# Rotary embedding on one core: 8 MB tiles of sixteen sequence rows per partition in place of 2 MB tiles of four

## Chip, cores, metric

One core of one Trainium2 chip runs the whole program. The metric is the device time of one execution in microseconds (us), as a median of several. The kernel before took 163.36 us (163.12 to 163.46, 4 runs). Profiled spans are 1.7 to 1.8 us shorter than the device time in every run whose record lists both; a span runs from the first to the last recorded instruction or transfer.

## The reference

The input x is [16, 512, 16, 64] (batch, sequence, head, dim) in float32, 33.55 MB. Only the first half of dim is rotated, by cos and sin tables of [512, 32], of which only the first 16 columns are used. The second half is copied.

```python
x1, x2 = x[..., :32], x[..., 32:]
c, s = cos[..., :16], sin[..., :16]          # broadcast over batch and head
first  = x1[..., :16] * c - x1[..., 16:] * s
second = x1[..., :16] * s + x1[..., 16:] * c
out = concatenate([first, second, x2], axis=-1)
```

33.55 MB must be read and 33.55 MB written. There are four vector products or sums per tile.

## The kernel before

One batch is one tile of 2 MB: sequence rows 4p to 4p+3 lie in partition p, so each partition's run in memory is 4 x 16 x 64 x 4 B = 16 KB. Six tiles can be resident. Products go to separate buffers `a_t` and `b_t`; the sums go back into the tile, and the tile is stored as it lies. The tables are expanded over heads by GpSimd at the start.

```python
x_pool  = tile_pool(name="xp",  bufs=6)      # 6 x 16 KB per partition
ab_pool = tile_pool(name="abp", bufs=4)
# ... GpSimd expands cos, sin to CCX, SSX [P, 4, H, 2, Q] ...
for b in range(B):                            # 16 tiles
    x_t = x_pool.tile([P, K, H, D], fp32)
    nc.sync.dma_start(out=x_t, in_=xf[b])                      # load, SP queue
    nc.vector.tensor_mul(out=a_t, in0=x12, in1=cc_op)          # 128 x 2048
    nc.vector.tensor_mul(out=b_t, in0=x12, in1=ss_op)          # 128 x 2048
    nc.vector.tensor_tensor(out=x12[.., 0:Q], in0=a_t[.., 0:Q], in1=b_t[.., Q:2*Q], op=subtract)  # 128 x 1024
    nc.vector.tensor_tensor(out=x12[.., Q:2*Q], in0=a_t[.., Q:2*Q], in1=b_t[.., 0:Q], op=add)     # 128 x 1024
    nc.scalar.dma_start(out=of[b], in_=x_t)                    # store, ACT queue
```

## Time and profile before

| | before |
|---|---|
| device time | 163.36 us |
| span | 161.4 us |
| bytes moved, mean rate | 67.25 MB, 417 GB/s |
| vector engine busy | 108.7 us (67%) |
| 2 MB load, median from issue to landing | 20.3 us |
| 2 MB store, the same | 23.4 us |

Lines of the page (the profiler's summary of one run) of before. DVE is the vector engine and POOL is GpSimd; SPq and ACTq are the queues from which loads and stores are issued; L64 is line 64 of the kernel. The issue of a DMA is when its queue starts it, its landing is when all of it has arrived. The lines are: busy time by engine, the rows of the span cut into 40 slices (a digit is the busy share in tenths; GB/s is what the DMA engines moved), two groups of vector instructions (busy us and mean ns of one, then the idle time before them), and the DMA issues (KB each, median us from issue to landing).

```profile
DVE 108.7 (67%) x64; POOL 6.0 (4%) x14
...
DVE  0009999999995692947839296592957939389400
...
DMA  5999999999999999999999999999999999999994
GB/s 162 430 414 447 414 382 443 414 430 447 418 434 434 422 443 430 418 451 422 426 443 422 430 434 430 434 434 418 447 422 426 451 414 428 439 422 438 430 422 195
...
L65 DVE TENSOR_TENSOR b_t<-x_t,SSX 128x2048 f32<-128x2048 f32 x16 | 36.5, 2283 | 0.0
L66 DVE TENSOR_TENSOR x_t<-a_t,b_t 128x1024 f32<-128x1024 f32 x16 | 19.5, 1220 | 0.2
...
x_t<-in_x_dram SPq DMA_DIRECT2D x16, 2048.0 KB, 20.3
out_dram<-x_t ACTq DMA_DIRECT2D x16, 2048.0 KB, 23.4
```

The DMA row is full from the second slice to the last but one, while the vector row has gaps. The table of windows (start:end, length, vector busy, GpSimd busy, clock, DMA share, GB/s) says at what rate:

```profile
5.00:6.00 1.00, 0.00 (x0) 0.00 (x0) 1.00 1.02 434
...
25.00:40.00 15.00, 14.93 (x10) 0.00 (x0) 1.00 1.00 430
...
140.00:150.00 10.00, 8.15 (x6) 0.00 (x0) 1.00 1.01 431
...
156.00:158.00 2.00, 0.00 (x0) 0.00 (x0) 1.00 0.95 410
```

It is about 430 GB/s with loads only (5 to 6 us), with both directions (25 to 150 us), and near that with stores only (156 to 158 us; the two windows before it have 451 and 426). 67.25 MB at 0.432 MB/us is 156 us of the 161.4 us span. The waits of the vector engine (engine, line, waited for: us in total, times, longest) are for loads and are short, but for the first one, of 11.9 us, which is for the expanded tables:

```profile
DVE a_t L64 <- DMA x_t<-in_x_dram: 30.1, 10, 3.2
DVE a_t L64 <- POOL CCX L49: 11.9, 1, 11.9
```

So the kernel is at the rate of the DMA engines, with a ramp at the start and a last landing at the end.

### The profile page before, as it was taken

How to read it: one execution, taken by the hardware profiler on the slowest of the kernel's cores; microseconds unless marked ns; L12 is line 12 of the kernel's file. 1: busy time of each engine (PE TensorE's matmuls, PEld its weight loads, DVE VectorE, ACT ScalarE, POOL GpSimd, SP SyncE). 2: the span in 40 equal slices, each digit the busy share in tenths (PEclk: the TensorE clock that was granted, in tenths of full speed). 3: DMA queues.
4: the chain of work that ended last, by engine and by line, in shares of the span. 5: the costliest groups of instructions: out<-in, count | busy, mean ns of one | idle time of the engine just before them, and what ended most of it. 6: DMA issues, size and time to landing. Idle time of an engine off the chain costs nothing.

```text
span 161.4 us, 189 instructions
## 1 busy us (share of the span) xinstructions
DVE 108.7 (67%) x64; POOL 6.0 (4%) x14
## 2 busy tenths in 40 slices
DVE  0009999999995692947839296592957939389400
POOL 3090000000000000000000000000000000000000
DMA  5999999999999999999999999999999999999994
GB/s 162 430 414 447 414 382 443 414 430 447 418 434 434 422 443 430 418 451 422 426 443 422 430 434 430 434 434 418 447 422 426 451 414 428 439 422 438 430 422 195
DMA packets 4673, 67.25 MB, mean 417 GB/s; under 512 B 544, under 2 KB 544, under 8 KB 576
## 3 DMA queue, kind: packets, MB, share of 16 engines
q1 hardware_dynamic: 2304, 33.56, 49.4%
q10 hardware_dynamic: 2304, 33.56, 48.5%
q0 software_dynamic: 64, 0.13, 0.2%
q14 instruction: 1, 0.01, 0.0%
HBM read 33.69 MB, written 33.55 MB: 417 GB/s over the span
## 4 chain that ended last, share of the span: by engine, by line
DMA 60%; DVE 28%; POOL 2%; issue 2%; DVEq 1%; POOLq 0%; SPq 0%; PEldq 0%
DMA out_dram<-x_t 31%; DMA x_t<-in_x_dram 25%; DVE a_t L64 9%; DVE b_t L65 8%; DVE x_t L66 6%; DVE x_t L72 5%; DMA cosL<-in_cos_dram 4%; POOL CCX L49 1%; DVEq L105 1%; POOL SSX L50 1%; POOLq L105 0%; SPq L57 0%; DVEq L66 0%; PEldq L105 0%
## 5 line engine op out<-in xcount | busy, mean ns | idle before, releaser
L64 DVE TENSOR_TENSOR a_t<-x_t,CCX 128x2048 f32<-128x2048 f32 x16 | 37.0, 2313 | 42.1 <-DMA x_t<-in_x_dram 30.1
L65 DVE TENSOR_TENSOR b_t<-x_t,SSX 128x2048 f32<-128x2048 f32 x16 | 36.5, 2283 | 0.0
L66 DVE TENSOR_TENSOR x_t<-a_t,b_t 128x1024 f32<-128x1024 f32 x16 | 19.5, 1220 | 0.2
L72 DVE TENSOR_TENSOR x_t<-a_t,b_t 128x1024 f32<-128x1024 f32 x16 | 19.5, 1218 | 0.0
L49 POOL COPY CCX<-cosL 128x512 f32<-128x512 f32 x4 | 2.4, 612 | 5.4 <-DMA cosL<-in_cos_dram 5.4
L50 POOL COPY SSX<-sinL 128x512 f32<-128x512 f32 x4 | 2.4, 614 | 0.1
L39 POOL DMA_DIRECT2D cosL<-in_cos_dram x1 | 0.7, 668 | 0.8 <-PEq L105 0.8
L40 POOL DMA_DIRECT2D sinL<-in_sin_dram x1 | 0.5, 534 | 0.0
L94 POOL MEMSET const-float32-0.0<- 128x1 f32 x1 | 0.1, 98 | 0.2 <-issue 0.2
L94 POOL MEMSET const-bfloat16-1.0<- 128x1 bf16 x1 | 0.1, 101 | 0.0
L94 POOL MEMSET const-uint8-127<- 128x1 uint8 x1 | 0.1, 101 | 0.0
L94 POOL MEMSET const-float32-1.0<- 128x1 f32 x1 | 0.1, 98 | 0.0
## 6 DMA issues: line engine op xcount, KB each, us to landing
x_t<-in_x_dram SPq DMA_DIRECT2D x16, 2048.0 KB, 20.3
out_dram<-x_t ACTq DMA_DIRECT2D x16, 2048.0 KB, 23.4
cosL<-in_cos_dram POOLq DMA_DIRECT2D x1, 64.0 KB, 6.6
sinL<-in_sin_dram POOLq DMA_DIRECT2D x1, 64.0 KB, 7.1
```

The costliest lines, as they stand in the source:

```text
L39: nc.gpsimd.dma_start(out=cosL[:], in_=cosf)
L40: nc.gpsimd.dma_start(out=sinL[:], in_=sinf)
L49: nc.gpsimd.tensor_copy(out=dst_c, in_=src_c)
L50: nc.gpsimd.tensor_copy(out=dst_s, in_=src_s)
L64: nc.vector.tensor_mul(out=a_t[:], in0=x12, in1=cc_op)
L65: nc.vector.tensor_mul(out=b_t[:], in0=x12, in1=ss_op)
L66: nc.vector.tensor_tensor(out=x12[:, :, 0:Q], in0=a_t[:, :, 0:Q], in1=b_t[:, :, Q : 2 * Q], op=mybir.AluOpType.subtract,)
L72: nc.vector.tensor_tensor(out=x12[:, :, Q : 2 * Q], in0=a_t[:, :, Q : 2 * Q], in1=b_t[:, :, 0:Q], op=mybir.AluOpType.add,)
L94: nc = _bacc.Bacc("TRN2", target_bir_lowering=False, num_devices=1)
L105: with _tile.TileContext(nc) as tc:
```

## The change

Its intent is longer contiguous runs and fewer, larger transfers. Sixteen sequence rows per partition give runs of 64 KB and four tiles of 8 MB, of which three are resident (three slots). To make the room, the cos product is made in place and the sin product goes to PSUM, another on-chip memory, and the tables stay unexpanded over heads (a broadcast operand does it). The vector work is the same, in chunks of four rows.

```diff
-    K = S // P                                   # 4
+    K = 16
+    T = B * S // (P * K)                         # 4 tiles of 8 MB
-    x_pool = ... tile_pool(name="xp", bufs=6)
-    ab_pool = ... tile_pool(name="abp", bufs=4)
+    x_pool = ... tile_pool(name="xp", bufs=3)
+    b_pool = ... tile_pool(name="bp", bufs=2, space=PSUM)
     (cut: tables loaded on the ACT queue, copied by the vector engine to table[P, 2, K, 2, Q])
-    for b in range(B):
+    for t in range(T):
         x_t = x_pool.tile([P, K, H, D], fp32)
-        nc.sync.dma_start(out=x_t, in_=xf[b])
+        nc.sync.dma_start(out=x_t, in_=xf[t])
+        for k0 in range(0, K, 4):
+            x1 = x_t[:, k0:k0+4, :, 0:HF]
+            b_t = b_pool.tile([P, 4, H, HF], fp32)
+            nc.vector.tensor_mul(out=b_t, in0=x1, in1=s)
+            nc.vector.tensor_mul(out=x1, in0=x1, in1=c)
+            nc.vector.tensor_sub(out=x1[.., 0:Q],  in0=x1[.., 0:Q],  in1=b_t[.., Q:HF])
+            nc.vector.tensor_add(out=x1[.., Q:HF], in0=x1[.., Q:HF], in1=b_t[.., 0:Q])
-        nc.scalar.dma_start(out=of[b], in_=x_t)
+        nc.scalar.dma_start(out=of[t], in_=x_t)
```

More of the change, by code (lines that the diff above doesn't have):

```diff
@@ L20 @@
     fp32 = mybir.dt.float32
+    P = 128
     B, S, H, D = x.shape
@@ L24 @@
     HF = D // 2
-    P = 128
-    K = S // P
-    xf = x.rearrange("b (p k) h d -> b p (k h d)", p=P)
-    of = out.rearrange("b (p k) h d -> b p (k h d)", p=P)
-    cosf = cos.rearrange("(p k) j -> p (k j)", p=P)
-    sinf = sin.rearrange("(p k) j -> p (k j)", p=P)
-    const_pool = ctx.enter_context(tc.tile_pool(name="const", bufs=1))
-    x_pool = ctx.enter_context(tc.tile_pool(name="xp", bufs=6))
-    ab_pool = ctx.enter_context(tc.tile_pool(name="abp", bufs=4))
-    cosL = const_pool.tile([P, K, HF], fp32)
@@ L38 @@
-    sinL = const_pool.tile([P, K, HF], fp32)
-    nc.gpsimd.dma_start(out=cosL[:], in_=cosf)
-    nc.gpsimd.dma_start(out=sinL[:], in_=sinf)
-    CCX = const_pool.tile([P, K, H, 2, Q], fp32)
-    SSX = const_pool.tile([P, K, H, 2, Q], fp32)
-    for k in range(K):
-        dst_c = CCX[:, k].rearrange("p h c j -> p (h c) j")
-        dst_s = SSX[:, k].rearrange("p h c j -> p (h c) j")
-        src_c = cosL[:, k : k + 1, 0:Q].to_broadcast((P, 2 * H, Q))
-        src_s = sinL[:, k : k + 1, 0:Q].to_broadcast((P, 2 * H, Q))
-        nc.gpsimd.tensor_copy(out=dst_c, in_=src_c)
-        nc.gpsimd.tensor_copy(out=dst_s, in_=src_s)
@@ L52 @@
-    cc_op = CCX.rearrange("p k h c j -> p (k h) (c j)")
-    ss_op = SSX.rearrange("p k h c j -> p (k h) (c j)")
-    for b in range(B):
-        x_t = x_pool.tile([P, K, H, D], fp32)
-        nc.sync.dma_start(out=x_t.rearrange("p k h d -> p (k h d)"), in_=xf[b])
-        a_t = ab_pool.tile([P, K * H, HF], fp32)
-        b_t = ab_pool.tile([P, K * H, HF], fp32)
-        x12 = x_t.rearrange("p k h d -> p (k h) d")[:, :, 0:HF]
-        nc.vector.tensor_mul(out=a_t[:], in0=x12, in1=cc_op)
-        nc.vector.tensor_mul(out=b_t[:], in0=x12, in1=ss_op)
-        nc.vector.tensor_tensor(
-            out=x12[:, :, 0:Q],
-            in0=a_t[:, :, 0:Q],
-            in1=b_t[:, :, Q : 2 * Q],
-            op=mybir.AluOpType.subtract,
-        )
-        nc.vector.tensor_tensor(
-            out=x12[:, :, Q : 2 * Q],
-            in0=a_t[:, :, Q : 2 * Q],
-            in1=b_t[:, :, 0:Q],
-            op=mybir.AluOpType.add,
-        )
-        nc.scalar.dma_start(out=of[b], in_=x_t.rearrange("p k h d -> p (k h d)"))
+    K = 16
@@ new lines @@
+    T = B * S // (P * K)
+    PB = S // K
+    REP = P // PB
+    xf = x.rearrange("b s h d -> (b s h d)").rearrange("(t p f) -> t p f", t=T, p=P)
+    of = out.rearrange("b s h d -> (b s h d)").rearrange("(t p f) -> t p f", t=T, p=P)
+    cosf = cos.rearrange("(p k) j -> p (k j)", k=K)
+    sinf = sin.rearrange("(p k) j -> p (k j)", k=K)
+    const_pool = ctx.enter_context(tc.tile_pool(name="const", bufs=1))
+    x_pool = ctx.enter_context(tc.tile_pool(name="xp", bufs=3))
+    b_pool = ctx.enter_context(tc.tile_pool(name="bp", bufs=2, space=bass.MemoryType.PSUM))
@@ new lines @@
+    stage = const_pool.tile([PB, 2, K, HF], fp32)
+    nc.scalar.dma_start(out=stage[:, 0].rearrange("p k j -> p (k j)"), in_=cosf)
+    nc.scalar.dma_start(out=stage[:, 1].rearrange("p k j -> p (k j)"), in_=sinf)
+    table = const_pool.tile([P, 2, K, 2, Q], fp32)
+    for r in range(REP):
+        for t in range(2):
+            nc.vector.tensor_copy(
+                out=table[r * PB : (r + 1) * PB, t],
+                in_=stage[:, t, :, 0:Q].unsqueeze(2).to_broadcast((PB, K, 2, Q)),
+            )
@@ new lines @@
+    C = table[:, 0].rearrange("p k c j -> p k (c j)")
+    Sn = table[:, 1].rearrange("p k c j -> p k (c j)")
+    KC = 4
+    for t in range(T):
+        x_t = x_pool.tile([P, K, H, D], fp32)
+        nc.sync.dma_start(out=x_t.rearrange("p k h d -> p (k h d)"), in_=xf[t])
+        for k0 in range(0, K, KC):
+            x1 = x_t[:, k0 : k0 + KC, :, 0:HF]
+            c = C[:, k0 : k0 + KC].unsqueeze(2).to_broadcast((P, KC, H, HF))
+            s = Sn[:, k0 : k0 + KC].unsqueeze(2).to_broadcast((P, KC, H, HF))
+            b_t = b_pool.tile([P, KC, H, HF], fp32)
+            nc.vector.tensor_mul(out=b_t[:], in0=x1, in1=s)
+            nc.vector.tensor_mul(out=x1, in0=x1, in1=c)
+            nc.vector.tensor_sub(
+                out=x1[:, :, :, 0:Q], in0=x1[:, :, :, 0:Q], in1=b_t[:, :, :, Q:HF]
+            )
+            nc.vector.tensor_add(
+                out=x1[:, :, :, Q:HF], in0=x1[:, :, :, Q:HF], in1=b_t[:, :, :, 0:Q]
+            )
+        nc.scalar.dma_start(out=of[t], in_=x_t.rearrange("p k h d -> p (k h d)"))
```

## The prediction

> **What bounds the kernel now.** DMA throughput. The page shows 67.25 MB at a mean of 417 GB/s over a 161.4 us span, with the DMA row at 9 in all but the first and last of 40 slices. The table of windows gives 430 to 433 GB/s from 25 to 150 us, about the same when only loads run (434 to 438 at 5 to 10 us) and when only stores are left (about 430 at 150 to 158 us). 67.25 MB at 0.432 MB/us is 156 us; the rest is the ramp (flow starts in effect at 2.6 us) and the last landing. The vector engine is busy 108.7 us (67%) and waits for loads; its time costs nothing.
>
> **What the change removes, adds, moves.**
> - Bytes: unchanged. Runs go from 16 KB to 64 KB, but 432 GB/s already holds whether loads or stores run, so I expect no rate gain (within 2%).
> - Table building: GpSimd copies (until 11.95 us) become small vector copies, hidden behind the first 8 MB load. Worth 0.
> - Vector work: same elements, four ops of the same shapes per 2 MB chunk. From the timeline, four ops take 6.8 us start to start, 27.2 us per 8 MB. The Trainium skill ("Perfetto Trace Analysis", Optimizing Scalar/DVE Operations) gives a per-instruction overhead of ~60 ns on SBUF and ~125 ns on PSUM; no trace here shows it yet. Three of four ops touch PSUM: estimate 27.6 us per tile.
> - Granularity: the loss. The pipeline unit goes from 2 MB (4.85 us of DMA at 0.432 MB/us, 6.8 us of compute) to 8 MB (19.4 us, 27.6 us), with three slots for four tiles. No store can start before a whole tile has landed and been computed; the last load must wait for the first store.
>
> **Estimated schedule** (0.432 MB/us, shared equally by load and store when both are queued; 2 us from issue to flow, 1 us to landing). Equal sharing rests on the Trainium skill ("DMA: Bandwidth & Descriptors", Queues, rings and completion order): each engine round-robins between queues; the trace agrees roughly (median 20.3 us per load, 23.4 per store).
> - Load 0 lands 23.3, load 1 42.7. Compute 0 ends 50.9; store 0 shares with load 2 (lands ~70) and lands ~82.
> - Load 3 issues only then, shares with stores 1 and 2, lands ~123. Vector ends tile 2 at ~106, then waits ~17 us.
> - Compute 3 ends ~151; store 3 alone lands ~173.5; span ~174.
> - DMA is empty from ~139 to ~153 us, about 14 us.
> The chain is load 0, compute 0, store 0, load 3, compute 3, store 3. Slower vector ops count about once, not four times: delaying store 0 just lets load 2 finish first; only compute 3 counts in full. Reported time is 2 us over the span now, so 176 us.
>
> **Prediction: 176 us, 172 to 181. Faster by over 2%: 0.02; within 2%: 0.05; slower: 0.93.**
>
> **What would show each step.** First landing at 22 to 24.5 us. Vector busy 109 to 116 us, PSUM ops no more than ~0.1 us longer. In the chain of waits: one vector wait of 12 to 22 us for load 3, issued at the landing of store 0 (~80 to 84). In the 40 slices: DMA full until ~137, then 3 to 4 slices near zero, then stores alone for ~20 us.
>
> **What would make it wrong.** Unequal sharing: if stores got 55% of the shared stretch, load 3 lands ~128 and the time is ~180; at 45%, ~172. 64 KB runs changing the DMA rate (1% is ~1.2 us on the chain). PSUM operands at half rate: compute 3 alone adds 10 us or more. Stores of part of a tile starting early, which the code does not do, would hide the loss.

## The result, and the profile after

| | before | after |
|---|---|---|
| device time, median | 163.36 us (163.12 to 163.46) | 174.52 us (173.07 to 175.37) |
| span of the profiled run | 161.4 us | 173.4 us |
| mean DMA rate over the span | 417 GB/s | 388 GB/s |
| vector busy | 108.7 us | 110.2 us |

The ratio after to before is 1.0674 (95% interval 1.0619 to 1.0729). Ratios here are the mean time of one kernel's fast runs over that of the other's of the same rounds, so they are not quite the ratio of the medians quoted.

The page of after, the same parts:

```profile
DVE 110.2 (64%) x72; POOL 0.2 (0%) x4
...
DVE  0020459999999999999999990000199999900000
...
DMA  7996999599995999799996999969999700099595
GB/s 242 499 491 250 484 484 484 257 469 484 484 484 242 484 484 469 333 408 484 484 454 272 484 484 484 439 287 484 484 486 408 318 0 0 0 484 484 242 484 242
...
L64 DVE TENSOR_TENSOR b_t<-x_t,table 128x2048 f32<-128x2048 f32 x16 | 36.0, 2292 | 24.1 <-DMA x_t<-in_x_dram 24.1
L65 DVE TENSOR_TENSOR x_t<-x_t,table 128x2048 f32<-128x2048 f32 x16 | 35.9, 2283 | 0.0
L66 DVE TENSOR_TENSOR x_t<-x_t,b_t 128x1024 f32<-128x1024 f32 x16 | 19.4, 1211 | 0.0
...
stage<-in_cos_dram ACTq DMA_DIRECT2D x1, 64.0 KB, 10.2
x_t<-in_x_dram SPq DMA_DIRECT2D x4, 42.3
stage<-in_sin_dram ACTq DMA_DIRECT2D x1, 64.0 KB, 17.4
out_dram<-x_t ACTq DMA_DIRECT2D x4, 33.9
```

The vector instructions cost what they did: 2283 and 2292 ns against 2283, 1211 against 1220. The new thing is three slices without any DMA. (The GB/s row swings because each 64 KB packet, here one partition's run, is counted in one piece; a packet takes 2.4 us on its engine, and a slice is 4.3 us.) The windows around the hole, columns as before:

```profile
135.00:140.00 5.00, 5.00 (x5) 0.00 (x0) 1.00 0.49 210
140.00:145.00 5.00, 5.00 (x4) 0.00 (x0) 1.00 0.00 0
145.00:150.00 5.00, 5.00 (x5) 0.00 (x0) 1.00 0.00 0
150.00:155.00 5.00, 1.73 (x2) 0.00 (x0) 1.00 0.49 210
```

By the single packets in the trace, the last packet of store 2 ended at 139.7 us and the first of store 3 began at 152.6 us: 12.9 us without flow. The spans differ by 12.0 us. The hole is the loss, to within a microsecond.

The vector engine's waits for tiles show where it comes from:

```profile
DVE b_t L64 <- DMA x_t<-in_x_dram: 24.1, 2, 21.3
```

Two waits in all, one of 2.9 us for load 0 (the rest of the time before it went to waiting for tables) and one of 21.3 us for load 3. The chain that ended last, in order of time (start us, length us, what):

```profile
0.73 22.66 DMA x_t<-in_x_dram
...
50.40 31.39 DMA out_dram<-x_t
...
81.89 43.00 DMA x_t<-in_x_dram
```

Between the first two lies the compute of tile 0 (23.5 to 50.4 us). After the third comes the compute of tile 3 (125.0 to 151.7 us), during which only the rest of store 2 was left to move, and then store 3 alone. Load 3 could not be issued before 81.8 us because it needs the slot of tile 0, whose store landed then.

### The profile page after: what moved, and what is told of

Same layout as the page of the kernel before. It is cut to its first block, busy times and chain, and to the rows that moved or that the text cites. A ratio compares the mean times of both kernels' runs of the same rounds, so it can differ in the third digit from the quotient of the medians.

```text
span 173.4 us, 137 instructions
## 1 busy us (share of the span) xinstructions
DVE 110.2 (64%) x72; POOL 0.2 (0%) x4
## 4 chain that ended last, share of the span: by engine, by line
DMA 56%; DVE 29%; issue 2%; DVEq 1%; SPq 0%
DMA x_t<-in_x_dram 38%; DMA out_dram<-x_t 18%; DVE x_t L65 10%; DVE b_t L64 9%; DVE x_t L69 5%; DVE x_t L66 5%; DVEq L98 1%; DVEq L64 0%; SPq L58 0%
## 5 line engine op out<-in xcount | busy, mean ns | idle before, releaser
L64 DVE TENSOR_TENSOR b_t<-x_t,table 128x2048 f32<-128x2048 f32 x16 | 36.0, 2292 | 24.1 <-DMA x_t<-in_x_dram 24.1
L65 DVE TENSOR_TENSOR x_t<-x_t,table 128x2048 f32<-128x2048 f32 x16 | 35.9, 2283 | 0.0
L66 DVE TENSOR_TENSOR x_t<-x_t,b_t 128x1024 f32<-128x1024 f32 x16 | 19.4, 1211 | 0.0
L69 DVE TENSOR_TENSOR x_t<-x_t,b_t 128x1024 f32<-128x1024 f32 x16 | 19.4, 1211 | 0.0
L48 DVE COPY table<-stage 32x512 f32<-32x512 f32 x8 | 3.3, 416 | 17.4 <-DMA stage<-in_cos_dram 11.0
## 6 DMA issues: line engine op xcount, KB each, us to landing
stage<-in_cos_dram ACTq DMA_DIRECT2D x1, 64.0 KB, 10.2
stage<-in_sin_dram ACTq DMA_DIRECT2D x1, 64.0 KB, 17.4
```

The lines of the kernel that those rows point to most:

```text
L48: nc.vector.tensor_copy(out=table[r * PB : (r + 1) * PB, t], in_=stage[:, t, :, 0:Q].unsqueeze(2).to_broadcast((PB, K, 2, Q)),)
L64: nc.vector.tensor_mul(out=b_t[:], in0=x1, in1=s)
L65: nc.vector.tensor_mul(out=x1, in0=x1, in1=c)
L66: nc.vector.tensor_sub(out=x1[:, :, :, 0:Q], in0=x1[:, :, :, 0:Q], in1=b_t[:, :, :, Q:HF])
L69: nc.vector.tensor_add(out=x1[:, :, :, Q:HF], in0=x1[:, :, :, Q:HF], in1=b_t[:, :, :, 0:Q])
```

## The experiments

My theory after the result was granularity: one 8 MB tile must land, be computed and be stored in turn, and the last tile's chain is longer than the transfers left to hide it. The rivals were the vector form (PSUM, in place), the 64 KB runs in themselves, and the three slots in themselves. The fluid estimates quoted below are a small calculation with 0.432 MB/us shared by the two queues, 6.7 us of vector work per 2 MB chunk and about 1 to 2 us to start and to land. Its numbers come from the traces of before and after.

In all runs "before" was timed on the same chip in the same rounds, at 163.16 to 163.32 us. All results were correct unless it is said otherwise.

### e1_tile2mb: tile size and number of slots put back

```diff
-    K = 16
+    K = 4
-    x_pool = ... bufs=3
+    x_pool = ... bufs=6
```

> The changed kernel with only its tile size put back: four rows per partition, 2 MB tiles, 16 KB runs, six resident; in-place cos products, sin products in PSUM and vector-built tables stay. Granularity theory (the loss is that one 8 MB tile must land, be computed and be stored in turn): 161 to 164 us, DMA full in all slices but the ends, as before. Rival (the vector form, PSUM or in-place, costs the time): stays near 174 us. Vector busy about 110 us either way.

Measured: 163.00 us, ratio 0.9984 (0.9967 to 1.0001), vector busy 108.8 us, DMA row full. The rest of the change (PSUM, in-place products, unexpanded tables built on the vector engine) costs nothing. The whole loss lies in the tiles: their size, their three slots in place of six, and their longer runs, all of which this run puts back at once. The next runs take these apart.

### e3_run16k: 8 MB tiles with 16 KB runs

Each tile holds four batches, so a DMA still moves 8 MB, but each partition's runs are 16 KB and so are the packets.

```diff
-    xf = x...rearrange("(t p f) -> t p f", t=T, p=P)
+    xf = x.rearrange("(t g) (p k) h d -> t p g (k h d)", g=4, p=P)
     (the same for the output; tables of four rows)
```

> The changed kernel with 8 MB tiles and three slots kept, but each tile is four batches with 16 KB runs per partition, so DMA packets of 16 KB in place of 64 KB. Granularity theory: unchanged, 173 to 177 us, the same wait of about 21 us for load 3. Rival (64 KB runs make the transfers or the sharing between the queues worse): clearly below, 164 to 169 us. The sin table, which landed at 18.6 us behind 64 KB packets, should land before 10 us, without effect on the time.

Measured: 175.97 us, ratio 1.0786 (1.0754 to 1.0817). The wait for load 3 is 22.6 us. The long runs are not the loss; they even give about 1% back (174.5 against 176.0 us; the intervals of the two ratios to before do not meet, but the runs are of different rounds, so I put no weight on it). The sin table landed at about 14.5 us, not before 10 us as I expected: in this run each table is loaded as 128 packets of 512 B, in after as 32 of 2 KB, so it needs four times as many turns. The chain:

```profile
49.91 32.41 DMA out_dram<-x_t
...
82.41 43.27 DMA x_t<-in_x_dram
```

### e4_pieceload and e4_piecestore: one side in four parts

```diff
 # e4_pieceload                                       # e4_piecestore
-  nc.sync.dma_start(out=x_t, in_=xf[t])             -  nc.scalar.dma_start(out=of[t], in_=x_t)
+  for k0 in (0, 4, 8, 12):                          +  inside the chunk loop, after the add:
+      nc.sync.dma_start(out=x_t[:, k0:k0+4],        +      nc.scalar.dma_start(out=of[t][:, part],
+          in_=xf[t][:, part])                       +          in_=x_t[:, k0:k0+4])
```

> The changed kernel with each 8 MB load issued as four loads of 16 KB per partition into the same tile; three slots and whole 8 MB stores stay. Granularity theory by a fluid estimate (0.432 MB/us, equal sharing, 6.7 us of vector work per piece): compute of a tile runs while its own later pieces land, store 0 issues near 36 us instead of 50, the last store near 132 instead of 152, about 162 us. Rival (three slots, the last load waiting for the first store, are the loss in themselves): 172 to 176 us, since that wait remains.

> The changed kernel with each 8 MB store issued as four stores of 16 KB per partition, each after its quarter is computed; whole loads and three slots stay. Fluid estimate: the last quarter's store is a quarter as long (172 less about 15 us at the end), but the earlier stores slow load 2 and load 3 then lands near 130 instead of 125: about 167.5 us. Rival (only the last store matters): 159 to 162 us. Rival (slots alone): 172 to 176 us.

Measured: e4_pieceload 173.33 us (167.52 to 176.67), e4_piecestore 163.01 us, ratio 0.9991 (0.9957 to 1.0025). **Both estimates failed, in opposite directions.** The four runs of e4_pieceload are spread widely; the profile is of a slow one. So I compare no times with it. The chain of e4_piecestore, and the issue of its stores (first issue, time to the last, count):

```profile
50.47 31.30 DMA out_dram<-x_t
...
81.83 28.26 DMA x_t<-in_x_dram
```

```profile
34.87 102.44 ACTq L72 DMA_DIRECT2D out_dram<-x_t  x16
```

Load 3 was issued at the same moment as in the changed kernel (81.8 us) and landed after 28.3 us instead of 43.0. With equal sharing that is not possible while stores are queued. I counted the packets that began on each queue in a stretch where both had work, and those from the first to the last start of a packet of load 3:

```
                 stretch    load packets   store packets  |  while load 3 moved: load, store packets, its share of bytes
after            87-116 us  97 of 64 KB    95 of 64 KB    |  128, 101   0.56
e3_run16k        54-60 us   79 of 16 KB    79 of 16 KB    |  512, 492   0.51
e4_piecestore    54-60 us   32 of 64 KB    32 of 16 KB    |  128,  96   0.84
e4_pieceload     54-60 us   31 of 16 KB    32 of 64 KB    |  (loads in four parts, not one stretch)
```

The DMA engines take packets from the two queues in turn, one for one, whatever their size. (The 0.56 of after comes mostly from the ends of its count, which are a packet per engine, 16 packets, wide.) A packet here is one partition's contiguous run. So where both queues have work, bytes are shared as the packet sizes: equal in after and in e3_run16k, about four to one for loads in e4_piecestore, one to four in e4_pieceload. My fluid estimates had used equal sharing for all. This became the packet theory, and the next runs test it.

### e4_pieceboth: both sides in four parts

The two edits above together.

> The changed kernel with loads and stores both in four parts of 16 KB per partition, three 8 MB slots, whole slots released. Packets equal, so equal sharing; both ends fine-grained. Fluid estimate: 162 us, DMA full throughout. If the packet theory is wrong and pieced loads are bad in themselves (e4_pieceload took 173 us): 168 us or more.

Measured: 163.34 us, ratio 0.9998 (0.9980 to 1.0016), DMA row full. Pieced loads are not bad in themselves. With packets equal, fine grain at both ends removes the loss although the three 8 MB slots stay.

### f1_run16k_piecestore: early stores, equal packets

Run e3_run16k with the stores of e4_piecestore: `nc.scalar.dma_start(out=of[t][:, k0 // 4], in_=x_t[:, k0:k0+4])` in the chunk loop.

> Run e3_run16k (8 MB tiles, 16 KB runs on loads and stores) with the four-part stores of e4_piecestore: stores start as early as there, but load and store packets are now of equal size. Packet theory (the queues alternate packet by packet, so bytes are shared as the packet sizes; in e4_piecestore the loads had 64 KB against 16 KB, four fifths of the flow): load 3 lands near 130 us as the equal-sharing estimate said, 166 to 169 us. Rival (starting the stores early is all that helped e4_piecestore): 162 to 164 us.

Measured: 163.40 us, ratio 1.0007 (0.9990 to 1.0023). **The time is the rival's, not that of the estimate.** The sharing was equal as the packet theory says: 512 load packets against 448 store packets while load 3 moved, which therefore took 41.5 us, not 28:

```profile
50.60 30.26 DMA out_dram<-x_t
...
80.92 41.47 DMA x_t<-in_x_dram
```

The estimate was wrong for another reason, which I argue from the trace and have not tested. It started the first store when the first chunk was done, at about 30 us. In the program the chunks are interleaved in pairs, so the first store was issued at 35.0 us, the loads kept the whole flow for longer, and load 3 landed at 122.4 us instead of 130. The stores of the first half of tile 3 then came just in time: store packets ran on without a hole (previous ones until 140.4 us, the next from 139.8 us). So early stores are enough by themselves, without unequal packets.

### f2_latepieces: an experiment that did not do what it said

```diff
-        nc.scalar.dma_start(out=of[t], in_=x_t)
+        for k0 in (12, 8, 4, 0):
+            nc.scalar.dma_start(out=of[t][:, part], in_=x_t[:, k0:k0+4])
```

> The changed kernel with the four-part stores issued from the last quarter to the first, so no store starts before the whole tile is computed, as in the changed kernel, but store packets are 16 KB against load packets of 64 KB. Packet theory: loads get four fifths, load 3 lands near 108 us in place of 125, the stores' backlog covers the last compute, 161 to 164 us. Rival (early stores helped): 173 to 176 us, since nothing starts earlier.

Measured: 163.17 us, ratio 0.9999 (0.9955 to 1.0043). It looks like a hit, but it is void: stores were reordered when the program was built, and the first was issued when the first chunk was ready, as in e4_piecestore:

```profile
34.92 104.71 ACTq L73 DMA_DIRECT2D out_dram<-x_t  x16
```

### g3_store16k: late stores with small packets

Each store DMA takes two quarters that are not neighbours, so its runs stay 16 KB and it needs both pairs of chunks.

```diff
-        nc.scalar.dma_start(out=of[t], in_=x_t)
+        ov = of[t].rearrange("p (a b f) -> p b a f", a=2, b=2)
+        xv = x_t.rearrange("p (a b k) h d -> p b a (k h d)", a=2, b=2)
+        for b in range(2):
+            nc.scalar.dma_start(out=ov[:, b], in_=xv[:, b])
```

> A valid form of f2_latepieces, whose stores turned out to start early after all. The changed kernel, but each tile's store is two DMAs, quarters 0 and 2, then 1 and 3, so each needs the last pair of chunks (first store near 48 us instead of 50) while its packets are 16 KB; loads keep 64 KB packets. Packet theory: loads get four fifths of the flow, load 3 lands near 108 to 111 us, the last compute ends near 137 and the stores' backlog lasts that long: 161 to 165 us. Rival (only stores that start early remove the loss): 172 to 176 us.

Measured: 162.76 us, ratio 0.9973 (0.9947 to 0.9999). Here the stores were late (first issue 48.5 us), and still the hole is gone. The DMA row, the chain, the store issues and the wait for load 3:

```profile
DMA  7969799799799799999999997997999999999993
```

```profile
50.77 31.38 DMA out_dram<-x_t
...
82.23 29.32 DMA x_t<-in_x_dram
```

```profile
48.51 90.46 ACTq L75 DMA_DIRECT2D out_dram<-x_t  x8
111.64 4.50 DVE L64 TENSOR_TENSOR b_t<-x_t,table 128x2048 f32<-128x2048 f32 x2 [7.57 <-DMA x_t<-in_x_dram]
```

Load 3 was issued at the same time as in after and landed at 111.6 us, 13.3 us earlier (128 load packets of 64 KB against 111 store packets of 16 KB while it moved, 0.82 of the bytes). The stores that were held back for it then filled the time of the last compute: packets of the earlier stores until 139.9 us, of the last tile's from 139.3 us. Nothing was finer in the loads or the compute. The stores were also in two parts, the first of which was issued 2.3 us before the second (for the last tile at 136.2 and 138.4 us). That is not what closes the hole: by an estimate, a whole store issued at 138.4 us would have started at 139.3 us (in after the first packet came 0.9 us after the issue), before the earlier packets ended; and load 3 was issued no earlier than in after. So the run length of the stores, 16 against 64 KB, decides about 12 us here, through the order in which bytes move and not through the rate.

### f5_nocos and g1_sinhalf: less and more vector work

```diff
 # f5_nocos (wrong result on purpose)          # g1_sinhalf (result unchanged)
-  nc.vector.tensor_mul(x1, x1, c)               nc.vector.tensor_mul(b_t, x1, s)
                                              +  if k0 % 8 == 0: nc.vector.tensor_mul(b_t, x1, s)
```

> The changed kernel without the in-place cos product (the result is wrong on purpose): 2.2 us less vector work per 2 MB chunk, 8.9 us less per tile. If vector time counts once on the chain, as predicted (an earlier store 0 only shares with load 2 for longer): 164.5 to 168 us (fluid estimate 166). If it counts for tiles 0 and 3 both: 162 us or less. If vector time is off the chain, as in the kernel before: 173 to 176 us.

> The changed kernel with the sin product computed twice in every other chunk (result unchanged): 4.4 us more vector work per tile. If vector time counts once on the chain, as the prediction put it: 178 to 180 us. Fluid estimate with the measured equal shares: 175 to 176 us, because a later store 1 leaves load 3 more of the flow, so load 3 lands 4 us earlier and takes back what the longer last compute costs. If it counts twice (tiles 0 and 3): 183 us.

Measured: f5_nocos 167.03 us, ratio 1.0225 (1.0206 to 1.0244); its result is wrong. g1_sinhalf 174.70 us, ratio 1.0704 (1.0673 to 1.0736). Taking away 8.9 us per tile gains 7.5 us against the 174.52 us of after; adding 4.4 us per tile costs 0.2 us, within the spread (the intervals of the two ratios to before overlap); that is just under the fluid estimate of 175 to 176 us and far from the 178 us or more of the prediction's rule. The chains of f5_nocos and then of g1_sinhalf:

```profile
41.59 40.06 DMA out_dram<-x_t
...
81.74 43.98 DMA x_t<-in_x_dram
```

```profile
55.22 26.63 DMA out_dram<-x_t
...
81.95 37.70 DMA x_t<-in_x_dram
```

Store 0 lands at the same time, 81.7 to 81.9 us, whether it was issued at 41.6, 50.4 or 55.2 us: by then three loads and one store have moved, and the DMA engines were busy all along. With less vector work load 3 still takes 44 us, so only the last compute gets shorter. With more of it, stores 1 and 2 are queued later, load 3 has more of the flow (37.7 us instead of 43.0) and gives back what the longer last compute costs.

### e6_twoslots and e2_tile4mb: slots and size

```diff
 # e6_twoslots                     # e2_tile4mb
-    bufs=3                        -    K = 16, bufs=3
+    bufs=2                        +    K = 8,  bufs=6
```

> The changed kernel with two resident tiles in place of three: load 2 must wait for store 0 and load 3 for store 1. Fluid estimate: 187 us (load 2 lands 109, load 3 136 us, DMA empty for about 12 us more). If slots played no part: 174 to 176 us.

> The changed kernel with eight rows per partition: 4 MB tiles, 32 KB runs, six resident (the same 192 KB per partition). Fluid estimate: no empty DMA, 161 to 164 us. If the loss grew in step with the tile (11 us for four times the size): 166 to 169 us.

Measured: e6_twoslots 186.42 us, ratio 1.1428 (1.1406 to 1.1451), with a second hole in its DMA row:

```profile
DMA  6999998790099996979999988599998895059995
```

e2_tile4mb 163.21 us, ratio 0.9994 (0.9971 to 1.0018). With the same memory in slots of half the size, nothing of the loss is left: it is not in step with the tile size.

No version beat both kernels clearly. g3_store16k is the fastest at 0.9973 of before, which counts as the same.

## Why the prediction was right, and where it was not

- **What bounds the kernel, and the bytes: right.** DMA engines at 430 GB/s before; longer runs brought no rate. In after, the windows of 84 to 100 and 100 to 120 us have 393 and 465 GB/s, together 433 GB/s over the 36 us in which load 3 and stores 1 and 2 moved.
- **The time: right.** 174.52 us against 176 (172 to 181). The span is 173.4 us against about 174, and the device time lies 1.7 us above it, not 2.
- **The schedule: right in each step.** Load 0 landed at 23.4 us (predicted 23.3), compute 0 ended at 50.4 (50.9), store 0 landed at 81.8 (~82), load 3 at 124.9 (~123), compute 3 ended at 151.7 (~151), and DMA was empty for 12.9 us (~14). The vector engine's wait for load 3 was 21.3 us, more than the ~17 named but inside the 12 to 22.
- **Vector cost: right, with a term too large.** I took 27.6 us per tile from a PSUM overhead (12 operations at the 65 ns that lie between the two cited figures would have made it 28.0); measured were 26.7 us per tile (from 125.0 to 151.7 us), less than the 27.2 us of before. PSUM as an operand cost nothing to be seen.
- **Tables "worth 0": right, with little margin.** The small table loads share the DMA engines with 64 KB packets, so the sin table came 17.4 us after its issue. It was expanded 2.9 us before load 0 landed. With an earlier first tile it would have held everything up:

```profile
18.57 2.04 DVE L48 COPY table<-stage 32x512 f32<-32x512 f32 x5 [6.33 <-DMA stage<-in_sin_dram]
23.49 4.50 DVE L64 TENSOR_TENSOR b_t<-x_t,table 128x2048 f32<-128x2048 f32 x2 [2.87 <-DMA x_t<-in_x_dram]
```

- **"Slower vector ops count about once ... only compute 3 counts in full": wrong upward.** It holds for less work (f5_nocos: 7.5 us for 8.9), but 4.4 us more per tile cost 0.2 us (g1_sinhalf), because load 3 then lands 5.2 us earlier.
- **"Equal sharing": right for this kernel, for a reason I did not have.** The prediction cited the Trainium skill ("DMA: Bandwidth & Descriptors", Queues, rings and completion order) for turns between queues; that section says that an engine drains a whole packet before it switches. The traces agree with the turns (97 load packets against 95 store packets in after), but I took turns to mean equal bytes, and the traces show bytes shared as the packet sizes (0.82 to 0.84 for loads with runs four times as long). It was equal only because loads and stores had the same run length. The check in the prediction, 20.3 us per load and 23.4 per store before, could not tell this either, for the same reason.
- **"Stores of part of a tile starting early would hide the loss": right** (e4_piecestore and f1_run16k_piecestore, 163.0 and 163.4 us).

What stays open: why the runs of e4_pieceload range over 9 us. No run gave the 8 MB tiles a fourth slot, so tile size and number of slots are not separated for them: by an estimate with 0.432 MB/us, equal shares and 26.7 us of compute, load 3 would land near 110 us, its compute end near 137 us and the earlier stores near 138 us, which leaves no hole. What is shown is that whole 8 MB tiles in three slots make the hole, and that finer ends, smaller tiles in more slots, or shorter runs on the stores each remove it.

## What to carry to other kernels

When a kernel is at the DMA rate, bigger tiles have little to gain (4 and 8 MB brought nothing here) and can lose: work out when the last load lands, and whether the transfers left by then last as long as the last tile's compute; if not, the difference is a hole in the DMA row (12.9 us here, none with half the tile and twice the slots). When loads and stores share the DMA engines, the side with longer runs gets more of the flow, in the ratio of the packets, and here shorter runs on the side that can wait (16 against 64 KB) gave the other side priority at no cost in rate (g3_store16k took the whole 11 us back). Check in the profile that an edit of issue order really took effect before reading its time.

## What the Trainium skill lacked or had wrong

- "DMA: Bandwidth & Descriptors", Queues, rings and completion order: it says that engines turn between queues packet by packet, and gives a packet as some 9 to 17 descriptors. It does not say what this does to the shares in bytes, nor how many bytes a packet of a DMA issued from SP or ACT has. Here a packet was one partition's run of 16, 32 or 64 KB (611 ns for 16 KB, 2418 ns for 64 KB), turns were one for one (32 against 32 packets of 64 and 16 KB), and a load got 0.82 to 0.84 of the bytes with runs four times as long.
- No page has what that means for small transfers: a 64 KB table load next to a load with 64 KB packets took 10.2 and 17.4 us to land, next to one with 16 KB packets 4.7 and 7.1 us (after and e4_pieceload, both with 32 packets of 2 KB per table). With 128 packets of 512 B per table it took 8.0 and 13.2 us next to 16 KB packets (e3_run16k): both the number of turns and the size of the other queue's packets count.
- "Perfetto Trace Analysis", Optimizing Scalar/DVE Operations: about 60 ns of overhead on SBUF and 125 ns on PSUM. Sums with one PSUM source took 1211 ns, those with both in SBUF 1220 ns; products into PSUM 2292 ns, into SBUF 2283 ns. No run shows the extra.
- "SBUF — State Buffer", Summary: rules for kernel authors, has "Use 128 partitions; one DMA, not several" for a DMA-bound transfer. One 8 MB DMA in place of four of 2 MB cost 6.7% here, and splitting the stores gave it back (e4_piecestore). The rule needs beside it the pipeline around the transfer.
